# A planner that holds two engines for steps about to fall due, in a macaron encoder trunk on one core

## The chip, the cores and the metric

One core of one Trainium2 chip runs the whole program as one launch. The metric is the device time of an execution in microseconds (us), the median of several runs; the kernel before takes 918.53 us (three runs, 918.42 to 918.54). A core has five engines with an instruction queue each: TensorE (PE in the profile, its weight loads PEld), VectorE (DVE), ScalarE (ACT), GpSimd (POOL) and SyncE (SP, which here only issues DMAs). Each queue runs in its own order; semaphores hold an instruction until what it needs is there.

## The reference, cut to what matters

Two layers of a post-norm encoder on x of 1 x 256 x 1024 float32. Each layer is a SwiGLU, a mixer, a SwiGLU, each followed by a residual sum and a layer norm. The mixer of layer 0 is a bidirectional mLSTM with an output gate, that of layer 1 is windowed attention with 16 query heads on 4 key heads, a sink logit and a distance bias.

```python
def swiglu(x, w_in, w_out):                      # w_in 1024 x 5632, w_out 2816 x 1024
    gu = x @ w_in
    g, u = gu[..., :D_FF], gu[..., D_FF:]
    return (jax.nn.silu(g) * u) @ w_out
...
    p = x @ w_in                                 # mLSTM: q, k, v, o and the gates of both directions
...
    h = h_f + h_b                                # both directions, four heads of 256
    mu = jnp.mean(h, axis=-1, keepdims=True)
    var = jnp.mean(jnp.square(h - mu), axis=-1, keepdims=True)
    h = (h - mu) * lax.rsqrt(var + LN_EPS)
    h = h.transpose(0, 2, 1, 3).reshape(B, S, D_MODEL) * norm_g
    out = jax.nn.sigmoid(o.astype(jnp.float32)) * h
    return out.astype(x.dtype) @ w_out
...
for l in range(DEPTH):
    x = layer_norm(ALPHA * x + 0.5 * swiglu(x, ffn_w_in[l, 0], ffn_w_out[l, 0]), ...)
    x = layer_norm(ALPHA * x + mixer(x), ...)    # mLSTM for l = 0, attention for l = 1
    x = layer_norm(ALPHA * x + 0.5 * swiglu(x, ffn_w_in[l, 1], ffn_w_out[l, 1]), ...)
```

## The kernel before

**Arithmetic.** Every product of float32 matrices is made of three matmuls on a rounded part and its remainder: `mm3` (line 540) adds hi x hi, hi x lo and lo x hi. So each piece of a weight, a *word* of 128 partitions x 1024 numbers (512 KB), is loaded by `word` (493) on SP's queue and then split by `split` (502): ScalarE copies it to `w_hi`, VectorE subtracts to get `w_lo`. Activations are split in the same way when they leave PSUM (`split_evac`, 545). The 256 tokens are two tiles, t = 0 and 1.

**Stages.** `ffn`, `mlstm`, `ffn`, `ffn`, `attn`, `ffn`, each a function that writes down steps. An FFN does its first 768 hidden columns directly and the other 2048 in four *sevens* (`seven`, 844), each of which makes a 2 x 2 block product from seven products; some of their sums of words are made by DMAs that add (`bring`, issued by GpSimd), some by VectorE. All stages end in `tail` (650): the output projection, a residual sum, and the norm (`Norm`, 606), in which GpSimd takes a power for the column `rs`. The next stage is handed a `pending` that turns the normed x with the identity on TensorE (`to_xT`, 584) and splits it into `xT`.

**The head.** x is loaded in four quarters on ScalarE's queue (563), then ScalarE loads its table. TensorE turns the identity 14 times as a warm-up (`warm`, 592), turns the first quarter of x, warms up 8 times more and starts the first matmuls (`first_mm`, 725), between which the other quarters are turned. Steps for the sums of x that the sevens need (`x_sum`, named S) are made early, by VectorE and ScalarE. GpSimd works from the start on what it can: small loads of gates and sinks (`small_loads`, 572, issued by GpSimd), zeros, and the distance matrix of attention (`fwd`, `back`, `dist`), which takes four selects and an addition.

**The order of work.** Nothing of this is issued directly. `Book.note` writes each step down with what it depends on, `cost` gives it a duration, `latest` a due time (TensorE's own sequence laid end to end, and every other step as late as its users allow), and `sequence` (331) makes a list schedule: TensorE keeps the written order, the other four engines pick again and again. An engine's candidates are its 16 steps of earliest due time whose inputs are planned. Each has a time at which it could start (engine free, inputs there, a free slot), and the pick is:

```python
                soon = min(times)[0] + 1.0
                pick = min((x for x in times if x[0] <= soon), key=lambda x: x[1])
```

that is, of those that can start at once the one that is due first; an engine never idles while something can start. The planner's times decide only the order in each queue and which slot a tile takes. Slots are few: `HOMES` (line 29) has 10 for `w_hi`, 10 for `w_lo`, 16 for raw words and other big tiles, 8 PSUM banks.

**The mLSTM's end** (1124 to 1158). Four heads follow one another as `scores`, `mix`, `divide`, `settle`; `settle` normalizes a head's h, and its power is GpSimd's `hrs`. Between the heads stand the matmuls of the output gate, 32 units of three matmuls: 2 token tiles, 2 column halves m, 8 rows of blocks k. The eight gate words are indexed by (m, k // 2). The first four places, one a head, take token tile 0 with both halves, 4 units each; tile 1 follows in portions of 4, 4, 6 and 2. Then `gate_out` multiplies, `to_xT_banks` (a plain call of `to_xT`) turns h, and `tail` begins.

**Attention** (`attn`) interleaves, over 11 steps, `scores`, `scale`, `turn` and `values` of eight pairs of heads with pieces of projections. `values` sums into a bank that is emptied by the split into `q_hi` (ScalarE) and `q_lo` (VectorE).

Of the kernel before, what the change touches and what calls it, by code (L numbers as in the profile page):

```python
# [45 lines left out]
CT = [0, 1]  # L46

# [6 lines left out]
QUEUED = 6000.0  # L54

# [112 lines left out]
class Book:  # L168
# [162 lines left out]
    def sequence(self):  # L331
# [21 lines left out]
        dma = 0.0  # L353
# [20 lines left out]
        while len(given) < len(steps):  # L374
            best = None
            for e, list_ in todo.items():
# [7 lines left out]
                for n in cands:  # L384
                    s = steps[n]
                    t = max(free[e], ready[n])
                    if e == "SP":
                        t = max(t, dma - QUEUED)
                    t = homes(s, t)
                    if t is not None:  # L390
                        times.append((t, s.due, n))
                if not times:
                    continue
                soon = min(times)[0] + 1.0
                pick = min((x for x in times if x[0] <= soon), key=lambda x: x[1])
# [4 lines left out]
            s = steps[n]  # L400
# [10 lines left out]
            if e == "PE":  # L411
                at += 1
            else:
                todo[e].remove(n)
# [24 lines left out]
        self.given = given  # L439

# [13 lines left out]
def trunk_kernel(ctx: ExitStack, tc: tile.TileContext, x, ffn_w_in, ffn_w_out, ln_g, ln_b, ml_w_in, ml_gate_b,  # L454
# [24 lines left out]
    def bank(shape=(128, 512), name="pw"):  # L479
        return nc.tile(name, shape, "bank")  # L480
# [82 lines left out]
    for t, h in ((0, 0), (1, 0), (0, 1), (1, 1)):  # L563
        s_ = slice(h * 512, h * 512 + 512)
        nc.scalar.dma_start(xt[t][:, s_], x[0, t * 128:(t + 1) * 128, s_])
# [121 lines left out]
    def ffn(l, i, n, pending, last):  # L687
# [21 lines left out]
        if start:  # L709
            warm(14)  # L710
            to_xT(0, xt[0], (0,), nc.vector.tensor_copy)
# [4 lines left out]
        if start:  # L716
            gu(0)
            warm(8)
# [6 lines left out]
        def first_mm(ps, a):  # L725
# [5 lines left out]
            if a == 1:  # L731
                for t in range(2):
                    to_xT(t, xt[t], (1,))
# [211 lines left out]
    def mlstm(l, n, pending, last):  # L945
# [200 lines left out]
        to_xT_banks(0, flat[0])  # L1146
        wide_mm(po1[1], 1, wg, 1, range(6, 8))
        sigm(1, 1, po1[1])
        nc.scalar.preload_act_table(AF.Silu)
        for m in range(2):  # L1150
# [7 lines left out]
                    lambda: to_xT_banks(1, flat[1]))  # L1158

    def to_xT_banks(t, src):  # L1160
        to_xT(t, src)
# [219 lines left out]
```

## Time and profile before

| | |
|---|---|
| median of 3 runs | 918.53 us (918.42 to 918.54) |
| the profiled execution | 918.53 us, its span 916.8 us |
| granted TensorE clock | 0.997 |
| busy in the span | PE 904.0, DVE 810.7, ACT 584.5, POOL 144.3 us |
| DMA | 208.54 MB, mean 227 GB/s |

The profile is one execution. A timeline row gives start, duration, engine, line, operation, what is written and read (out<-in), shapes, how many such in a row, and in brackets how long the engine was idle before and what ended that. Since every step is issued from one line, all rows say L450, and the tiles' names tell them apart: `w_hi`, `w_lo` the parts of a word, `raw` and `b` words as loaded, `x` the tokens, `xT` the turned tokens, `S` the sums of x, `h` the mLSTM's output, `sc`, `pr` and `nse` scores, their turned form and their statistics in attention, `q` in attention also the result of a pair of heads. PE's durations overlap, as matmuls are pipelined, so starts are compared. A row of a stretch gives, after its length, busy time and count for PE, PEld, DVE, ACT and POOL, then the granted clock, the share of DMA time, and GB/s. A row of the list of waits gives who waited for whom: us in total, times, longest.

### The profile page before, as it was taken

How to read it: one execution, taken by the hardware profiler on the slowest of the kernel's cores; microseconds unless marked ns; L12 is line 12 of the kernel's file. 1: busy time of each engine (PE TensorE's matmuls, PEld its weight loads, DVE VectorE, ACT ScalarE, POOL GpSimd, SP SyncE). 2: the span in 40 equal slices, each digit the busy share in tenths (PEclk: the TensorE clock that was granted, in tenths of full speed). 3: DMA queues.
4: the chain of work that ended last, by engine and by line, in shares of the span. 5: the costliest groups of instructions: out<-in, count | busy, mean ns of one | idle time of the engine just before them, and what ended most of it. 6: DMA issues, size and time to landing. Idle time of an engine off the chain costs nothing.

```text
span 916.8 us, 12617 instructions
## 1 busy us (share of the span) xinstructions
PE 904.0 (99%) x4459; PEld 757.4 (83%) x4459; DVE 810.7 (88%) x985; ACT 584.5 (64%) x793; POOL 144.3 (16%) x177
## 2 busy tenths in 40 slices
PE   8999999999999999999999999999999999999996
PEld 7888888889988888888888888888898888888885
DVE  7989999887797989999889899997888698999985
ACT  6666777547564657776646667775488555677750
POOL 6112111005011021212011121210013202111100
PEclk9999999999999999999999999999999999999998
DMA  9998998944194688998965989989553367999831
GB/s 313 386 265 203 306 290 253 307 159 153 68 348 147 204 197 252 286 248 255 359 217 169 241 212 319 273 244 332 173 160 101 120 202 151 263 282 234 291 70 47
DMA packets 100704, 208.54 MB, mean 227 GB/s; under 512 B 6904, under 2 KB 21264, under 8 KB 100640
## 3 DMA queue, kind: packets, MB, share of 16 engines
q1 hardware_dynamic: 82368, 173.04, 53.7%
q0 software_dynamic: 17696, 33.65, 21.5%
q10 hardware_dynamic: 576, 1.05, 0.3%
q8 instruction: 35, 0.57, 0.2%
q14 instruction: 29, 0.24, 0.1%
HBM read 206.65 MB, written 1.05 MB: 227 GB/s over the span
## 4 chain that ended last, share of the span: by engine, by line
PE 94%; DVE 3%; ACT 1%; issue 1%; DMA 0%; DVEq 0%; ACTq 0%
PE pw L450 60%; PE py L450 34%; DVE w_lo L450 1%; DMA x<-in_x_dram 0%; ACT sc L450 0%; DVE x L450 0%; ACT w_hi L450 0%; DVE h L450 0%; ACT pr L450 0%; DVE pr L450 0%; DVE sc L450 0%; DVE few L450 0%; DVE xT_lo L450 0%; DVE hst L450 0%; DVE a_lo L450 0%
## 5 line engine op out<-in xcount | busy, mean ns | idle before, releaser
L450 ACT CAST w_hi<-b 128x1024 fp32r<-128x1024 f32 x224 | 234.2, 1056 | 88.1 <-PE py L450 44.5
L450 DVE TENSOR_TENSOR w_lo<-b,w_hi 128x1024 fp32r<-128x1024 f32 x224 | 267.1, 1218 | 17.6 <-ACT w_hi L450 17.1
L450 ACT CAST w_hi<-raw 128x1024 fp32r<-128x1024 f32 (+1 forms) x181 | 186.8, 1047 | 94.6 <-PE py L450 61.1
L450 DVE TENSOR_TENSOR w_lo<-raw,w_hi 128x1024 fp32r<-128x1024 f32 (+1 forms) x181 | 216.8, 1216 | 24.5 <-ACT w_hi L450 23.8
L450 PE MATMUL pw<-w_hi,xT_hi 128*128 128x512 f32 x480 | 189.5, 396 | 0.0
L450 PE MATMUL pw<-w_lo,xT_hi 128*128 128x512 f32 x480 | 186.5, 390 | 0.7 <-DVE w_lo L450 0.7
L450 PE MATMUL pw<-w_hi,xT_lo 128*128 128x512 f32 x480 | 187.0, 391 | 0.0
L450 PE MATMUL pw<-w_hi,S 128*128 128x512 f32 x512 | 162.9, 389 | 0.0
L450 POOL DMA_DIRECT2D b<-in_ffn_w_in_dram x64 | 77.3, 1210 | 457.7 <-DVE b L450 213.0
L450 PE MATMUL py<-w_hi,h_hi 128*128 128x512 f32 x317 | 125.2, 395 | 0.0
L450 PE MATMUL py<-w_hi,h_lo 128*128 128x512 f32 x317 | 123.8, 391 | 0.0
L450 PE MATMUL py<-w_lo,h_hi 128*128 128x512 f32 x317 | 123.5, 390 | 0.0
L450 PEld LDWEIGHTS pw<-w_hi,S 128*128 128x128 f32 x512 | 96.1, 188 | 20.0
L450 PEld LDWEIGHTS pw<-w_hi,xT_lo 128*128 128x128 f32 x480 | 90.0, 188 | 19.5 <-DVE xT_lo L450 0.3
L450 PEld LDWEIGHTS pw<-w_lo,xT_hi 128*128 128x128 f32 x480 | 90.3, 188 | 19.1 <-DVE w_lo L450 1.4
L450 PEld LDWEIGHTS pw<-w_hi,xT_hi 128*128 128x128 f32 x480 | 90.1, 188 | 17.3
L450 PE MATMUL pw<-w_lo,S 128*128 128x512 f32 x256 | 99.6, 389 | 0.0
L450 DVE TENSOR_TENSOR b<-b,b 128x1024 f32<-128x1024 f32 x64 | 78.1, 1221 | 2.0 <-DMA b<-in_ffn_w_in_dram 0.8
L450 PEld LDWEIGHTS py<-w_hi,h_lo 128*128 128x128 f32 x317 | 59.5, 188 | 13.2 <-DVE h_lo L450 0.7
L450 PEld LDWEIGHTS py<-w_lo,h_hi 128*128 128x128 f32 x317 | 59.6, 188 | 11.9
L450 PEld LDWEIGHTS py<-w_hi,h_hi 128*128 128x128 f32 x317 | 59.6, 188 | 11.6
L450 PEld LDWEIGHTS pw<-w_lo,S 128*128 128x128 f32 x256 | 48.1, 188 | 9.9
(198 smaller groups left out, 1076.2 us busy)
## 6 DMA issues: line engine op xcount, KB each, us to landing
b<-in_ffn_w_in_dram SPq DMA_DIRECT2D x128, 512.0 KB, 6.9
raw<-in_ffn_w_out_dram SPq DMA_DIRECT2D x88, 512.0 KB, 6.9
b<-in_ffn_w_in_dram POOLq DMA_DIRECT2D x64, 512.0 KB, 8.5
raw<-in_ffn_w_in_dram SPq DMA_DIRECT2D x32, 512.0 KB, 7.6
raw<-in_ml_w_in_dram SPq DMA_DIRECT2D x24, 512.0 KB, 8.6
raw<-in_ffn_w_in_dram SPq DMA_DIRECT2D x32, 256.0 KB, 6.1
raw<-in_at_w_in_dram SPq DMA_DIRECT2D x12, 512.0 KB, 8.4
raw<-in_ml_w_out_dram SPq DMA_DIRECT2D x8, 512.0 KB, 3.8
```

The source lines that it names most:

```text
L450: getattr(engines[s.engine], s.name)(*[real(x) for x in s.args], **{k: real(x) for k, x in s.kw.items()})
```

## The change

Five edits; the computation stays the same.

1. **Pressing steps.** For VectorE and ScalarE the pick goes through `wait_for`. If a step that is due earlier than the pick will be able to start before the pick would end (by more than 50 ns), and the pick would end later than that step's due time plus TensorE's present lateness less 500 ns, and the pick itself would not be made late by waiting, then the engine takes a step that ends by then (at most 60 ns over), or, if none does, stays idle for the pressing step.
2. **x on SP.** x's quarters are loaded on SP's queue, the same one as the words, written at the place where they are used: first quarter, first word, second quarter, then the second word and the last two. The warm-ups are 8 before the first turn of x and 14 after it.
3. **GpSimd late.** In the plan, a step of GpSimd other than an adding DMA does not start earlier than 25 us before it is due. This includes the small loads, the zeros and the distance matrix.
4. **The gate word by word.** The 32 units are listed anew: m = 0 for both tiles, word by word; then m = 1 for tile 0 and for tile 1. `GATE` says how many are taken at each place: 4 a head, 4 before the last `mix`, 10 after it, 2 after the turn of h's first tile.
5. `to_xT_banks` is replaced by the `to_xT` that it called.

```diff
+GATE = [4, 4, 4, 4, 4, 10, 2]
...
+PRESSING = 500.0
+EARLY = 25000.0
...
+                    if e == "POOL" and "accum_op" not in s.kw:
+                        t = max(t, s.due - EARLY)
...
-                soon = min(times)[0] + 1.0
-                pick = min((x for x in times if x[0] <= soon), key=lambda x: x[1])
+                now = min(times)[0]
+                open_ = [x for x in times if x[0] <= now + 1.0]
+                pick = min(open_, key=lambda x: x[1])
+                if e in ("DVE", "ACT"):
+                    pick = self.wait_for(times, open_, pick, now, late)
...
             if e == "PE":
                 at += 1
+                late = t - s.due
...
+    def wait_for(self, times, open_, pick, now, late):
+        steps = self.steps
+        takes = steps[pick[2]].takes
+        for u in sorted(times, key=lambda x: x[1]):
+            if u[1] >= pick[1]:
+                break
+            if now + 1.0 < u[0] < now + takes - 50.0 and now + takes > u[1] + late - PRESSING and (
+                    pick[1] + late > u[0] + steps[u[2]].takes + takes):
+                fits = [x for x in open_ if now + steps[x[2]].takes <= u[0] + 60.0]
+                return min(fits, key=lambda x: x[1]) if fits else u
+        return pick
...
-    for t, h in ((0, 0), (1, 0), (0, 1), (1, 1)):
+    def load_x(t, h):
         s_ = slice(h * 512, h * 512 + 512)
-        nc.scalar.dma_start(xt[t][:, s_], x[0, t * 128:(t + 1) * 128, s_])
+        nc.sync.dma_start(xt[t][:, s_], x[0, t * 128:(t + 1) * 128, s_])
+
+    load_x(0, 0)
...
         if start:
-            warm(14)
+            warm(8)
             to_xT(0, xt[0], (0,), nc.vector.tensor_copy)
...
             gu(0)
-            warm(8)
+            load_x(1, 0)
+            warm(14)
...
             if a == 1:
+                gu(1)
                 for t in range(2):
+                    load_x(t, 1)
                     to_xT(t, xt[t], (1,))
...
-        po = [bank(), bank()]
+        po = {}
+
+        def gate_units(n_):
+            for _ in range(n_):
+                t, m, k = units.pop(0)
+                if k == 0:
+                    po[t, m] = bank()
+                wide_mm(po[t, m], t, wg, m, (k,))
+                if k == 7:
+                    sigm(t, m, po[t, m])
+
+        units = [(t, 0, 2 * a + j) for a in range(4) for t in range(2) for j in range(2)]
+        units += [(t, 1, k) for t in range(2) for k in range(8)]
         nc.scalar.preload_act_table(AF.Sigmoid)
         for h in range(4):
-            wide_mm(po[h // 2], 0, wg, h // 2, range(4 * (h % 2), 4 * (h % 2) + 4))
+            gate_units(GATE[h])
             scores(h)
...
-        po1 = [bank(), bank()]
-        sigm(0, 0, po[0])
-        wide_mm(po1[0], 1, wg, 0, range(4))
+        gate_units(GATE[4])
         mix(3)
-        sigm(0, 1, po[1])
-        wide_mm(po1[0], 1, wg, 0, range(4, 8))
         divide(3)
         settle(3)
+        gate_units(GATE[5])
         for m in range(2):
             gate_out(0, m)
-        sigm(1, 0, po1[0])
-        wide_mm(po1[1], 1, wg, 1, range(6))
-        to_xT_banks(0, flat[0])
-        wide_mm(po1[1], 1, wg, 1, range(6, 8))
-        sigm(1, 1, po1[1])
+        to_xT(0, flat[0])
+        gate_units(GATE[6])
```

More of the change, by code (lines that the diff above doesn't have):

```diff
@@ L352, in sequence @@
         free = {e: 0.0 for e in todo}
-        dma = 0.0
+        dma = late = 0.0
         given = []
@@ L1157, in mlstm @@
         return tail(y, lambda c, t: pair(xT, A, c, tok(t)), (todo, todo), True, norm, last, 4,
-                    lambda: to_xT_banks(1, flat[1]))
-    def to_xT_banks(t, src):
-        to_xT(t, src)
+                    lambda: to_xT(1, flat[1]))
     def attn(l, n, pending, last):
```

## The prediction

> **What bounds the kernel.** I read the page first, then the list of who waited for whom on TensorE, then stretches of the span, and last the timelines around each wait that the list names.
>
> ```profile
> span 916.8 us, 12617 instructions
> PE 904.0 (99%) x4459; PEld 757.4 (83%) x4459; DVE 810.7 (88%) x985; ACT 584.5 (64%) x793; POOL 144.3 (16%) x177
> ```
>
> The profiled execution took 918.53 us, the same as the median of the three runs, so 1.7 us lie outside its span and the sum below can be made on the span and carried over unchanged. TensorE is idle for 916.8 - 904.0 = 12.8 us. A change that leaves the matmuls alone, as this one does, can only win from those.
>
> ```profile
> 57.73 5.44 PE pw L450 x24
> PE py L450 <- DVE ident L450: 1.7, 1, 1.7
> PE pw L450 <- DVE q_lo L450: 1.2, 2, 0.8
> PE pw L450 <- ACT pr L450: 0.7, 1, 0.7
> PE pw L450 <- DVE w_lo L450: 0.7, 1, 0.7
> PE py L450 <- DVE h L450: 0.5, 1, 0.5
> PE py L450 <- DVE xT_lo L450: 0.4, 1, 0.4
> PE py L450 <- DMA x<-in_x_dram: 0.3, 1, 0.3
> ```
>
> The first line is a piece of the chain that ended last, inside an FFN: 24 matmuls in 5.44 us, 0.227 us from start to start. That is the pace everything else is held against. The other seven are all of TensorE's waits. Two belong to the first 6 us. The other five are short, and they lie in three places: the head, the end of the mLSTM, the attention. The long FFN stretches have none. What the change can be worth is the sum of these five, with what each costs around its idle time.
>
> **The head.** Here four edits meet: x on SP's queue, warm-up split 8 and 14 for 14 and 8, GpSimd's work put off, the pressing rule.
>
> ```profile
> 1.72 3.25 PE L450 MATMUL py<-ident 128*128 128x128 f32 x14 [1.72 <-DVE ident L450]
> 5.23 1.12 PE L450 MATMUL py<-ident,x 128*128 128x128 f32 x4 [0.27 <-DMA x<-in_x_dram]
> 6.14 1.42 PE L450 MATMUL py<-ident 128*128 128x128 f32 x8
> 7.31 0.71 PE L450 MATMUL pw<-w_hi,xT_hi 128*128 128x512 f32 x2
> 7.86 0.64 PE L450 MATMUL py<-ident,x 128*128 128x128 f32 x4
> 8.26 0.70 PE L450 MATMUL pw<-w_hi,xT_lo 128*128 128x512 f32 x2
> 14.40 0.39 PE L450 MATMUL pw<-w_hi,xT_hi 128*128 128x512 f32 x1
> 15.44 0.50 PE L450 MATMUL pw<-w_lo,xT_hi 128*128 128x512 f32 x1 [0.65 <-DVE w_lo L450]
> 5.63 1.14 ACT L450 CAST w_hi<-raw 128x512 fp32r<-128x512 f32 x2 [0.99 <-DMA raw<-in_ffn_w_in_dram]
> 4.00:5.00 1.00, 0.96 (x5) 0.56 (x3) 0.00 (x0) 0.64 (x1) 0.69 (x3) 1.00 1.05 395
> ```
>
> Of x and the first word, x's quarter is now sent alone and the word behind it. Both together are 0.262 + 0.524 MB, and both orders have moved them by the time ScalarE now starts on the word, 5.63. So the word gains nothing, and freeing ScalarE of four issues gains nothing either, since it already sat 0.99 us waiting for that word. The quarter gains the time of the word: 0.524 MB at 395 GB/s (the stretch's last column) are 1.33 us, so it is there near 4.3 instead of 5.2.
>
> The other three quarters of x and the later words now stand in one order on SP; the engines move 395 GB/s whoever issues, so I take 0 for the words behind them.
>
> TensorE cannot use the earlier quarter. Four early transposes took 6.14 - 5.23 = 0.91 us, 0.228 each; four later ones 8.26 - 7.86 = 0.40, 0.10 each. The eight warm-ups took 7.31 - 6.14 = 1.17, which is three slow and five fast, so the rate changed near 6.8. After the change: transposes from 4.3 to 5.2, then 14 warm-ups that stand ahead of the first matmul in order: seven slow ones to 6.8, seven fast ones to 7.5. The first matmul starts 0.2 later than at 7.31. From both sides: 0.1 earlier if x lands as the eight warm-ups end (3.6, below), 1.1 later if all 14 stay slow (5.2 + 3.2 = 8.4).
>
> The stall further on is what can go. From 14.40 to 15.44 is 1.04 us for a step of 0.227, so 0.81 are lost.
>
> ```profile
> 10.11 1.64 DVE L450 TENSOR_TENSOR w_lo<-raw,w_hi 128x1024 fp32r<-128x1024 f32 x1 [0.26 <-ACT w_hi L450]
> 13.46 0.67 DVE L450 TENSOR_TENSOR S<-x,py 128x512 f32<-128x512 f32 x1
> 14.05 2.46 DVE L450 TENSOR_TENSOR w_lo<-raw,w_hi 128x1024 fp32r<-128x1024 f32 x2
> 9.35 1.32 POOL L450 TENSOR_SCALAR_AFFINE_SELECT fwd<-fwd 128x512 f32<-128x512 f32 x2
> L450 DVE TENSOR_TENSOR w_lo<-raw,w_hi x181: 681/1218/1635, 7.7 to 888.0; 128x1024 fp32r<-128x1024 f32 x179, 128x512 fp32r<-128x512 f32 x2
> 178.03 1.48 POOL L450 TENSOR_TENSOR rs<-rs,few 128x1 f32<-128x1 f32 x1 [29.80 <-DVE rs L450]
> ```
>
> VectorE took a sum S of no hurry (0.67) just ahead of the w_lo that TensorE stood waiting for, and an earlier w_lo took 1.64 instead of the median 1.218 beside GpSimd's select. Either repair, 0.42 or 0.67, covers most of 0.81, and the two together all of it. Head: -0.8 + 0.2 = **-0.6**.
>
> GpSimd's work is not saved, only put off to 25 us before it is due: the memsets and small loads for the mLSTM come shortly before 178.03, the selects and the addition for attention's distances some 25 us ahead of that stage. GpSimd's queue is in order, its loads included: behind the moved work stand the norms' rs, for which the next stage's x waits. The last row shows 29.80 us without work before such an rs, so I take nothing; without that cover an rs comes late by the pieces in front of it, 1.32 us for a pair of selects.
>
> At their new place the reading operations can hit VectorE as the select did: 0.42 each, five such (four selects, one addition), 0 to 2.1 us, hidden as long as VectorE runs ahead there. I take 0, since TensorE has no wait in the list before attention's own. [...]
>
> **The mLSTM's end.** The word-by-word order uses each of the first four gate words for both token tiles at once.
>
> ```profile
> 266.22 0.60 PE L450 MATMUL py<-ident,h 128*128 128x128 f32 x4
> 267.32 0.63 PE L450 MATMUL py<-ident,h 128*128 128x128 f32 x4 [0.50 <-DVE h L450]
> 269.41 0.39 PE L450 MATMUL py<-w_lo,xT_hi 128*128 128x512 f32 x1
> 270.22 0.50 PE L450 MATMUL py<-w_hi,xT_lo 128*128 128x512 f32 x1 [0.42 <-DVE xT_lo L450]
> 263.64 2.48 DVE L450 SCALAR_TENSOR_TENSOR w_lo<-raw,few,w_hi 128x1024 fp32r<-128x1024 f32 x2
> 267.09 2.48 DVE L450 SCALAR_TENSOR_TENSOR w_lo<-raw,few,w_hi 128x1024 fp32r<-128x1024 f32 x2
> 240.00:256.00 16.00, 16.00 (x106) 14.64 (x105) 12.24 (x34) 6.89 (x21) 1.44 (x2) 1.00 0.38 131
> 256.00:270.00 14.00, 13.30 (x71) 10.94 (x69) 13.84 (x28) 11.10 (x18) 3.33 (x2) 1.00 1.00 353
> ```
>
> Lost: 267.32 - 266.22 - 0.40 = 0.70, and 270.22 - 269.41 - 0.227 = 0.58, together 1.28. Both times VectorE was on a pair of w_lo of the output projection (2.48 us, to 266.1 and 269.6) when h or xT_lo came up. Why so late: all eight gate words are split early and stay live until token tile 1 has used them, which is 8 of 10 slots for hi and for lo. So VectorE idles 16.00 - 12.24 = 3.76 us in the first stretch and is full (13.84 of 14.00) in the second. In the new order one word is done with after each head, four slots come free by the end of the heads, and up to three splits (3.76 / 1.24) move into the idle time. Matmuls between the last mix and the transposes stay 10 units of three, 10 x 3 x 0.227 = 6.8 us of cover; the last four gate words, which were split before, must now be ready within them, and they take the slots freed. That is 3.7 us of relief for 1.28 us of stall: I take **-1.2**, between -1.3 and +0.7 (the first stall doubled, if those four words come late).
>
> **Attention.**
>
> ```profile
> 696.19 1.03 ACT L450 CAST w_hi<-raw 128x1024 fp32r<-128x1024 f32 x1
> 697.25 1.23 DVE L450 TENSOR_TENSOR w_lo<-raw,w_hi 128x1024 fp32r<-128x1024 f32 x1 [0.97 <-ACT w_hi L450]
> 698.40 0.42 DVE L450 TENSOR_TENSOR q_lo<-pw,q_hi 128x256 fp32r<-128x256 f32 x1
> 698.87 0.66 PE L450 MATMUL pw<-ident,sc 128*128 128x128 f32 x4 [0.80 <-DVE q_lo L450]
> 711.50 0.51 ACT L450 ACTIVATE sc<-sc,nse 128x256 f32<-128x256 f32 x1 [1.28 <-DVE nse L450]
> ```
>
> ScalarE begins a w_hi at 696.19 and VectorE its w_lo at 697.25, so q_lo, which frees the bank that TensorE wants, starts at 698.40. This is the case the new rule is written for: leave the long split, take the short step that is about to be ready, and even idle for it. Without the w_lo in front, q_lo starts up to 698.40 - 697.25 = 1.15 us earlier, more than the 0.80. What is queued behind the rule's waiting is that same w_lo, and TensorE's products with its word. Both q_lo waits, 1.2 in the list: **-1.2** (0 to -1.2). I leave the 0.7 on pr: there ScalarE itself idled 1.28 us for VectorE and the pr stood behind, an order made from planned durations that the chip did not keep. The last 0.7 can go too, or double.
>
> **Elsewhere** the FFNs have nothing to win; I charge +0.2 for the rule's idling.
>
> Sum: -0.6 - 1.2 - 1.2 + 0.2 = **-2.8**, span 914.0, time 918.53 - 2.8 = **915.7 us**.
>
> **Rivals.** *The plan's relief stays in the plan.* The rule acts on planned times; the row at 711.50 shows plan and chip apart by 1.28 us, more than most of these stalls. Then only what follows from the data flow comes, the gate words: -1.2, 917.3 us. Against it: the two q_lo stalls and the S ahead of w_lo are the plan's own choices, seen as such in the trace.
>
> *The clock comes later.* TensorE now idles from 1.72 + 8 x 3.25 / 14 = 3.6 to 4.3, against 0.27 before. The fast rate came 6.8 - 1.72 = 5.1 us after the first warm-up. If that count starts anew at 4.3, fast is 9.4: first matmul at 8.4, then 1.0 us at half rate, 0.5 lost; 8.4 - 7.31 + 0.5 = 1.6 instead of 0.2, so 915.7 + 1.4 = 917.1 us. For: the longer idle; against: x00 may be earlier, and 0.7 is short beside 5.1. [...]
>
> *VectorE idles itself into the bound: slower.* In the FFN's sevens there is little to idle with:
>
> ```profile
> 85.89:116.78 30.89, 30.89 (x142) 25.57 (x141) 29.62 (x30) 22.20 (x25) 4.82 (x5) 1.00 0.94 272
> ```
>
> One seven leaves VectorE 30.89 - 29.62 = 1.27 us, and the planner books a split at (1024 + 71) / 0.96 = 1.14 us where the trace has 1.218, so it believes in more. Waiting beyond 1.27 us in a seven falls on TensorE. Two waits of 0.9 (the rule allows up to a split less 0.05) are 1.8, 0.53 too many, in 16 sevens 8.5 us: 924.2 us. Against: the rule first looks for a step that fits, and does not wait if the split itself would be late.
>
> **Chances.** Forecast 0.49; relief in the plan only 0.27; clock 0.12; VectorE idling 0.12. A measurement of this kernel can tell about 0.2%, 1.84 us. The forecast is faster than that, the next two lie within it unless other gains come on top (0.06 of their 0.39), the last is slower: 0.55, 0.33, 0.12. Lower end 914.2: all five waits gone at no charge are 0.81 + 1.28 + 1.2 + 0.7 = 4.0, and 0.3 more if attention's cost more than their idle time, as the head's did (0.81 for 0.65). Upper end 918.6: the 917.3 of the first rival with one rs late by 1.3. Left out are the slower case and a tail.
>
> **What would show it.** Right: q_lo gone from TensorE's waits, the w_lo of the output projection spread over the heads, VectorE below 13.84 of 14 before the mLSTM's transposes, no 1.64 in the head, first matmul near 7.5. Wrong: slow transposes past 8 us; a new TensorE wait for w_lo inside an FFN; rs late with POOL busy ahead of it; the same waits at the same places.

## The result, and the profile after

The changed kernel takes 914.09 us (median of 5 runs, 913.66 to 914.60) against 918.53 (5 runs, 918.38 to 918.54): a ratio of 0.9952, 95% interval 0.9938 to 0.9967, so 4.44 us less, beyond the 0.2% that a measurement of this kernel can tell. The forecast was 915.7 with 914.2 to 918.6: the direction holds, the gain is 1.6 us larger than forecast, and the median lies 0.1 us below the lower end. The profiled execution of the changed kernel took 913.72 us.

The page's first lines and the whole list of TensorE's waits:

```profile
span 911.8 us, 12602 instructions
PE 902.6 (99%) x4459; PEld 757.3 (83%) x4459; DVE 811.4 (89%) x985; ACT 584.2 (64%) x793; POOL 145.4 (16%) x177
```

```profile
engine line waited for: us in total, times, longest us
PE py L472 <- DVE ident L472: 1.7, 1, 1.7
```

All engines do the work they did before. TensorE's idle time fell from 12.8 to 911.8 - 902.6 = 9.2 us, and of the list of seven only the wait for the identity at the very start is left. Idle time is 3.6 of the span's 5.0 us. The other 1.4 are busy time (904.0 to 902.6), which the prediction had put out of reach: the first matmul after a wait is longer than its neighbours (0.50 against 0.39 us in the rows of before), and the early transposes run at two rates, below.

**The head.** TensorE's timeline of the changed kernel (start, duration, operation, and the idle time ahead of it in brackets):

```profile
1.71 1.97 PE L472 MATMUL py<-ident 128*128 128x128 f32 x8 [1.71 <-DVE ident L472]
3.77 1.11 PE L472 MATMUL py<-ident,x 128*128 128x128 f32 x4
4.67 2.31 PE L472 MATMUL py<-ident 128*128 128x128 f32 x14
6.74 0.71 PE L472 MATMUL pw<-w_hi,xT_hi 128*128 128x512 f32 x2
...
13.66 0.39 PE L472 MATMUL pw<-w_hi,xT_hi 128*128 128x512 f32 x1
13.89 0.39 PE L472 MATMUL pw<-w_lo,xT_hi 128*128 128x512 f32 x1
```

x's first quarter is there at 3.77, not near 4.3, and TensorE hardly waits for it. The first matmul starts at 6.74 (7.31 before, 7.5 forecast). The product that came at 15.44 behind the stall comes at 13.89, 0.23 behind its neighbour: the stall is gone, and the head is 1.55 us shorter, not 0.6.

**The mLSTM's end.** The two stretches that the prediction quoted, and the transposes of h in TensorE's timeline, which now run in one piece:

```profile
240.00:256.00 16.00, 16.00 (x103) 14.48 (x102) 15.30 (x36) 9.44 (x27) 1.82 (x2) 1.00 0.75 239
256.00:270.00 14.00, 14.00 (x74) 11.87 (x73) 13.66 (x33) 9.21 (x15) 1.70 (x2) 1.00 0.94 320
```

```profile
264.37 1.04 PE L472 MATMUL py<-ident,h 128*128 128x128 f32 x8
266.86 0.39 PE L472 MATMUL py<-w_lo,xT_hi 128*128 128x512 f32 x1
267.09 0.40 PE L472 MATMUL py<-w_hi,xT_lo 128*128 128x512 f32 x1
```

VectorE (the third busy number) went from 12.24 to 15.30 of 16.00 in the first stretch: the splits moved forward as forecast. The second transpose group and the product behind xT_lo lost 0.72 and 0.61 us against their neighbours of before; both are given back, 1.33 together against 1.2 forecast.

**Attention.** TensorE where it waited for q_lo, then ScalarE and VectorE at the same place:

```profile
694.67 0.28 PE L472 MATMUL pw<-kT_hi,q_lo 64*128 64x256 f32 x2
694.88 0.66 PE L472 MATMUL pw<-ident,sc 128*128 128x128 f32 x4
```

```profile
693.07 1.03 ACT L472 CAST w_hi<-raw 128x1024 fp32r<-128x1024 f32 x1
694.39 0.42 DVE L472 TENSOR_TENSOR q_lo<-pw,q_hi 128x256 fp32r<-128x256 f32 x1 [1.23 <-ACT q_hi L472]
694.74 1.22 DVE L472 TENSOR_TENSOR w_lo<-raw,w_hi 128x1024 fp32r<-128x1024 f32 x1
```

This is the rule at work: VectorE idles 1.23 us, the last 0.3 of them with a split at hand (its `w_hi` was ready at 693.07 + 1.03 = 694.10), does q_lo, then the split; before, VectorE idled 0.97 us for `w_hi` and the split stood first. Both q_lo waits went (1.26 us), and the wait for pr as well (0.99 with what followed it), which the forecast had kept. ScalarE's rows for pr, before and in the changed kernel, show why:

```profile
713.00 0.56 ACT L450 CAST pr<-pw 128x512 fp32r<-128x512 f32 x1
706.27 1.20 ACT L472 CAST pr<-pw 128x512 fp32r<-128x512 f32 x2
```

Before, the second pr stood behind three steps on `sc` that had waited 1.28 us for VectorE (the row at 711.50 in the prediction). Now both stand ahead of such steps, the next of which starts at 708.07.

Two places got worse. The last pair's scores now wait for GpSimd's scaling. TensorE's and GpSimd's rows:

```profile
713.84 1.92 PE L472 MATMUL pw<-ident,sc 128*128 128x128 f32 x8
715.52 0.47 PE L472 MATMUL py<-w_hi,q_hi 128*128 128x512 f32 x1
```

```profile
713.11 1.84 POOL L472 TENSOR_SCALAR sc<-sc,nse 128x256 f32<-128x256 f32 x4 [4.02 <-DVE nse L472]
```

Eight transposes take 715.52 - 713.84 = 1.68 us here, where the eight of h above take 265.16 - 264.37 = 0.79 (the next product stands at 265.16): 0.89 us given back, in gaps of 0.12 us, too short for the list of waits. And at attention's entry GpSimd's postponed selects and the addition run beside VectorE. First VectorE in the kernel before, with GpSimd's addition where it stood before, then VectorE and GpSimd in the changed kernel:

```profile
12.99 1.31 POOL L450 TENSOR_TENSOR dist<-fwd,back 128x512 f32<-128x512 f32 x1
650.16 1.28 DVE L450 SCALAR_TENSOR_TENSOR x<-x,rs,ln_b 128x1024 f32<-128x1024 f32 x1
651.36 2.36 DVE L450 TENSOR_TENSOR w_lo<-raw,w_hi 128x1024 fp32r<-128x1024 f32 x2
653.97 1.22 DVE L450 TENSOR_TENSOR w_lo<-raw,w_hi 128x1024 fp32r<-128x1024 f32 x1
```

```profile
646.91 1.64 DVE L472 SCALAR_TENSOR_TENSOR x<-x,rs,ln_b 128x1024 f32<-128x1024 f32 x1
648.48 3.19 DVE L472 TENSOR_TENSOR w_lo<-raw,w_hi 128x1024 fp32r<-128x1024 f32 x2
651.92 1.97 DVE L472 TENSOR_TENSOR w_lo<-raw,w_hi 128x1024 fp32r<-128x1024 f32 x1
```

```profile
647.43 1.60 POOL L472 TENSOR_SCALAR_AFFINE_SELECT fwd<-fwd 128x512 f32<-128x512 f32 x1
648.99 1.60 POOL L472 TENSOR_SCALAR_AFFINE_SELECT back<-back 128x512 f32<-128x512 f32 x1
650.67 2.13 POOL L472 TENSOR_TENSOR dist<-fwd,back 128x512 f32<-128x512 f32 x1
```

VectorE loses 0.36 + 0.83 + 0.75 = 1.94 us, close to the 2.1 that the prediction gave as the upper bound. TensorE loses 0.6 us there against before: 0.2 at its first products near 642.6, and 0.4 near 654.5, where it stands for xT_lo (0.27) and then for the next product. Both are gone in f2_nopool and f2_again below, which differ from the changed kernel by GpSimd's lateness alone.

The operations of GpSimd are longer there as well: each of the two selects shown takes 1.60 us against 0.63 in the head of before (the pair at 9.35 us), the addition 2.13 against 1.31 (the first row above). Both engines are slower there; what makes them so was not shown.

### The profile page after: what moved, and what is told of

Read it like the earlier page. It is cut to its first block, busy times and chain, and to the rows that moved or that the text cites. A ratio compares the mean times of both kernels' runs of the same rounds, so it can differ in the third digit from the quotient of the medians.

```text
span 911.8 us, 12602 instructions
## 1 busy us (share of the span) xinstructions
PE 902.6 (99%) x4459; PEld 757.3 (83%) x4459; DVE 811.4 (89%) x985; ACT 584.2 (64%) x793; POOL 145.4 (16%) x177
## 4 chain that ended last, share of the span: by engine, by line
PE 93%; DVE 3%; ACT 1%; issue 1%; POOL 0%; DMA 0%; DVEq 0%; POOLq 0%
PE pw L472 60%; PE py L472 33%; DVE w_lo L472 1%; DVE x L472 1%; ACT sc L472 1%; DVE pr L472 0%; DMA x<-in_x_dram 0%; DVE stats L472 0%; ACT pr L472 0%; ACT w_hi L472 0%; POOL sc L472 0%; DVE xT_lo L472 0%; DVE sc L472 0%; DVE few L472 0%; POOL rs L472 0%
```

## The experiments

My theory after this comparison: each edit works in its own stage, the word-by-word gates in the mLSTM, x's landing at the start, the pressing rule in head and attention, GpSimd's lateness for the head and against attention's entry. The rival: the edits overlap, one of them does most of it. The table has all runs. "Head" is the start of the product that stood behind the stall (15.44 us in before), "rest" the time from there to the start of the last matmul, both in the profiled execution; "turn" is the start of the first transpose after the last slow one (0.21 us apart before it, 0.11 after). The ratio is to runs of the kernel before that were made along with each kernel (their medians are 918.44 to 918.53).

| kernel | us, median (range, runs) | ratio, 95% interval | turn | head | rest |
|---|---|---|---|---|---|
| before | 918.53 (918.38 to 918.54, 5) | | 6.78 | 15.44 | 893.64 |
| the whole change | 914.09 (913.66 to 914.60, 5) | 0.9938 to 0.9967 | 5.95 | 13.89 | 890.60 |
| e1_gate | 917.41 (917.33 to 917.61, 11) | 0.9980 to 0.9998 | 6.86 | 15.50 | 893.11 |
| e2_head | 918.45 (917.62 to 918.71, 11) | 0.9988 to 1.0006 | 6.68 | 15.46 | 893.75 |
| e3_press | 914.52 (914.43 to 914.68, 5) | 0.9944 to 0.9971 | 6.68 | 14.54 | 891.00 |
| e4_pool | 919.32 (918.67 to 920.95, 11) | 1.0006 to 1.0023 | 4.54 | 14.99 | 894.82 |
| f1_nopress | 917.05 (916.63 to 917.46, 11) | 0.9976 to 0.9994 | 7.55 | 15.60 | 892.73 |
| f2_nopool | 913.16 (912.85 to 915.28, 5) | 0.9936 to 0.9961 | 7.27 | 16.12 | 890.15 |
| f2_again | 913.74 (912.94 to 913.89, 5) | 0.9934 to 0.9959 | 6.44 | 14.76 | 889.97 |
| f3_warm | 913.80 (913.56 to 914.03, 5) | 0.9937 to 0.9962 | 4.54 | 13.74 | 890.62 |
| a_again | 914.12 (913.65 to 914.67, 5) | 0.9940 to 0.9965 | 7.52 | 14.88 | 890.58 |
| g1_scale | 913.38 (913.07 to 913.72, 5) | 0.9933 to 0.9958 | 5.24 | 14.56 | 890.07 |
| g3_scale_warm_pool | 913.14 (912.32 to 913.89, 5) | 0.9925 to 0.9952 | 6.03 | 15.35 | 889.54 |
| g4_scale_warm | 913.31 (913.06 to 913.46, 5) | 0.9931 to 0.9956 | 7.10 | 14.36 | 889.85 |
| f5_nohead | 913.90 (913.66 to 914.11, 5) | 0.9937 to 0.9964 | 4.75 | 13.72 | 890.68 |
| f6_nogate | 914.18 (913.84 to 915.32, 5) | 0.9943 to 0.9968 | 7.81 | 15.26 | 890.88 |

Two things bear on every row. In e4_pool, f1_nopress and f6_nogate no further transpose follows at once, so the turn is later than the number: 4.92, 8.28 and 8.32 by the record of the granted clock in the traces. And from the start of the last matmul to the end the span takes 7.7 us in before and e2_head, 7.3 in the other fourteen profiles: the other kernels have 0.43 us from there, whatever their edit.

### Each edit alone, on the kernel before

**e1_gate**: only the gates' order.

```diff
-            wide_mm(po[h // 2], 0, wg, h // 2, range(4 * (h % 2), 4 * (h % 2) + 4))
+            gate_units(GATE[h])
```

> The kernel before with the output gates of the mLSTM cut into word-by-word units, and nothing else. Theory (each edit acts in its own stage): the two TensorE waits in the mLSTM, which took 0.72 and 0.61 us more in before than in the changed kernel, go with the gates' order, since units of the gates fill the places where TensorE waited for the heads' powers; the time falls by 1.3 us, to 917.2, and head and attention stay as in before. Rival (the pressing rule did it: ScalarE's powers fell from 1.67 to 0.78 us of delay because engines kept time for them): the waits stay, the time stays within 0.3 us of 918.5.

Measured: 1.0 us gained, 1.3 expected, and 0.43 of it at the very end; in the mLSTM TensorE gained 0.6. The wait for h went, that for xT_lo stayed. Its TensorE rows of the head and of the mLSTM:

```profile
15.50 0.50 PE L451 MATMUL pw<-w_lo,xT_hi 128*128 128x512 f32 x1 [1.01 <-DVE w_lo L451]
...
266.26 1.04 PE L451 MATMUL py<-ident,h 128*128 128x128 f32 x8
...
269.68 0.50 PE L451 MATMUL py<-w_hi,xT_lo 128*128 128x512 f32 x1 [0.54 <-DVE xT_lo L451]
```

The first row tells something more. In this execution x landed 0.35 us earlier than in before's profile and the first matmul started at 7.16 instead of 7.31, with the head's code unchanged, and still the product came at 15.50: what is won ahead of the stall is lost in the stall (1.01 us of idle time instead of 0.65). In these executions VectorE sets the end of the head.

**e2_head**: only x on SP's queue, and 8 and 14 warm-ups.

```diff
-        nc.scalar.dma_start(xt[t][:, s_], x[0, t * 128:(t + 1) * 128, s_])
+        nc.sync.dma_start(xt[t][:, s_], x[0, t * 128:(t + 1) * 128, s_])
-            warm(14)
+            warm(8)
```

> The kernel before with the head's edit alone: x on SyncE's queue in order of use, and 8 and 14 warming matmuls in place of 14 and 8. The changed kernel ran the head 1.55 us earlier. Theory (x's landing, at 3.72 instead of 5.18, is worth only the start; the rest of the head is set by VectorE's and ScalarE's order, which the pressing rule and GpSimd's lateness change): the first matmul of the first layer comes 0.5 us earlier, but the wait of 0.8 us at 14.4 us stays, so that 0.3 to 0.6 us are gained: 918.0. Rival (the landing sets the whole head): 1.5 us are gained, 917.0, and the wait at 14.4 us is gone too.

Measured: no difference by the medians (918.45 and 918.45), but the eleven times fall into two groups, 917.62 to 917.78 (five) and 918.45 to 918.71 (six), where those of before lie at 918.40 to 918.73. The profile is one of the second group. Its TensorE rows:

```profile
4.07 1.12 PE L450 MATMUL py<-ident,x 128*128 128x128 f32 x4 [0.38 <-DMA x<-in_x_dram]
4.97 2.60 PE L450 MATMUL py<-ident 128*128 128x128 f32 x14
7.33 0.70 PE L450 MATMUL pw<-w_hi,xT_hi 128*128 128x512 f32 x2
...
15.46 0.50 PE L450 MATMUL pw<-w_lo,xT_hi 128*128 128x512 f32 x1 [0.83 <-DVE w_lo L450]
```

In this execution x is there 1.2 us earlier and nothing follows: the 14 warm-ups fill the time, as the prediction said, and the stall takes the rest. The rival's 917.0 was not reached. What made five executions 0.8 us shorter is not known, since none of them was profiled, so the edit's worth on the kernel before stays open between 0 and 0.8.

**e3_press**: only the planner's rule (the function that the change adds and its call).

```diff
+                if e in ("DVE", "ACT"):
+                    pick = self.wait_for(times, open_, pick, now, late)
```

> The kernel before with the planner's new rule for VectorE and ScalarE alone. Theory: it removes the waits for q_lo in the attention (0.88 and 0.38 us in before), most of those for pr (0.74 and 0.25) and the 0.8 us at 14.4 us, and does nothing to the first matmul; some 0.9 us come back as waits for GpSimd's scaled scores near 715 us: 2 us are gained, 916.5. Rival (the planner's own prices are off by more than the rule's 0.5 us, so that the relief stays on paper): within 0.4 us of 918.5, and the q_lo waits are still in the list.

Measured: 3.9 us gained, twice the theory's 2, nearly all that the whole change gains; without the 0.43 at the very end it is 3.5. All of TensorE's waits:

```profile
PE py L468 <- DVE ident L468: 1.7, 1, 1.7
PE py L468 <- DVE xT_lo L468: 0.4, 1, 0.4
PE pw L468 <- DVE w_lo L468: 0.2, 1, 0.2
```

Beyond the waits named in the theory, the one for h in the mLSTM is gone (0.5 us gained there), which I had put down to the gates. TensorE also gained 0.13 to 0.18 us at the end of each of the first three FFNs and at the start of the last one, 0.6 together; f1_nopress, without the rule, has none of it to speak of. The 0.9 us back at GpSimd's scaling near 715 are there as expected: the rule brings out that wait, not the lateness.

**e4_pool**: only GpSimd's lateness.

```diff
+                    if e == "POOL" and "accum_op" not in s.kw:
+                        t = max(t, s.due - EARLY)
```

> The kernel before with GpSimd's early work held until 25 us ahead of its due time, and nothing else. Theory: GpSimd's index and mask work leaves the first 15 us, in which one w_lo of VectorE took 1.64 us beside it and takes 1.23 without, so the wait at 14.4 us shrinks by 0.4; and it comes up at 646 to 653 us beside VectorE's x and w_lo steps, which costs 0.3 us there: within 0.3 us of 918.5. Rival (GpSimd's work never touched the path): the wait at 14.4 us stays 0.8 us and the attention's entry stays too. Rival (the late work hits harder): over 1 us lost at 640 to 660 us.

Measured: 0.9 us lost by the medians, more than the theory's bound of 0.3, less than the second rival's, and elsewhere. Here too the times fall into two groups, 918.67 to 919.32 (six) and 920.33 to 920.95 (five); the profile is of the first, at 918.98. The product behind the head's stall came 0.45 us earlier, the size expected, though the wait itself was no shorter (0.79 us), as TensorE's turn was early. The loss in the profile is in the mLSTM, where the plan, made anew, put one more scaled split ahead of the last head. TensorE's and VectorE's rows there:

```profile
268.43 0.63 PE L453 MATMUL py<-ident,h 128*128 128x128 f32 x4 [2.12 <-DVE h L453]
```

```profile
261.70 1.28 DVE L453 SCALAR_TENSOR_TENSOR w_lo<-raw,few,w_hi 128x1024 fp32r<-128x1024 f32 x1
262.89 0.87 DVE L453 SCALAR_TENSOR_TENSOR h<-py,den,h 128x256 f32<-128x256 f32 x2
```

In before the h step started at 261.78 with that split behind it; here it starts 1.1 us later, and the wait for h is 2.12 us in place of 0.50. A change of times anywhere in the plan can reorder a stage that was not touched.

### The whole change with one edit left out

**f1_nopress**: without the call of the rule.

```diff
-                if e in ("DVE", "ACT"):
-                    pick = self.wait_for(times, open_, pick, now, late)
```

> The changed kernel without the planner's new rule for VectorE and ScalarE; x, warming, GpSimd and gates as changed. Theory (the rule alone took 3.9 us, the rest together 0.5): the q_lo waits are back near 695 and 702 us, the wait for w_lo near 14 us too, while the mLSTM stays without waits for h and xT_lo: 917.6 to 918.3. Rival (the edits overlap, so that what the rule removes the others remove too): under 916.5.

Measured: 917.05, so that the rule is worth 914.1 to 917.05 = 2.9 us within the whole, below the theory's range by 0.5 us, far from the rival. Those of attention are the waits of before, the one for w_lo is half as long:

```profile
PE pw L470 <- DVE q_lo L470: 1.2, 2, 0.8
PE pw L470 <- ACT pr L470: 0.7, 1, 0.7
PE pw L470 <- DVE w_lo L470: 0.3, 1, 0.3
```

The mLSTM's waits do not come back: without the rule the other three edits clear them, while the rule alone (e3_press) cleared one.

**f2_nopool** and, for a second profile, **f2_again**: without GpSimd's lateness.

```diff
-                    if e == "POOL" and "accum_op" not in s.kw:
-                        t = max(t, s.due - EARLY)
```

> The changed kernel with GpSimd's work as early as before, all else as changed. Theory (GpSimd beside VectorE costs in both places): one w_lo of the head takes 1.64 us again and a wait of 0.3 to 0.6 us for w_lo is back near 14 us; the wait for xT_lo near 654 us, 0.27 us, is gone: 914.1 to 914.5. Rival (lateness is a plain loss, as the 0.9 us by which the kernel before grew with it alone would have it): 913.3. Rival (the head needs it wholly): 915.0.

> The changed kernel with GpSimd's work as early as before, once more, since its five times lay at 912.85 to 914.06 and at 915.28, and its profile, at 915.28, had the turn of TensorE's rate at 7.27 us and a wait of 1.05 us for w_lo at 14.85. Theory (early GpSimd work delays VectorE in the head, which matters when TensorE's turn is late, and saves some 0.4 us at 654 us): 912.8 where the turn comes by 6 us, 915 where it comes after 7, median near 913.5. Rival (lateness of GpSimd is a plain loss of 0.9 us): median 913.2 and no stall in the head at any turn.

Measured: nine of ten times from 912.85 to 914.06, one at 915.28, medians 913.16 and 913.74, against 914.09 and 914.12 with the lateness. In both profiles the rest is shorter by 0.4 to 0.6 us, because the 0.6 us at attention's entry are gone; the head is longer, 14.76 at a turn of 6.44 and 16.12 at 7.27, against 14.88 at 7.52 with the lateness. So both sides of the trade are real, as the theory had it, and the lateness looks like a loss of some 0.4 us (the medians of ten times are 913.7 and 914.1), which is less than the intervals can tell. The theory's 912.8 for an early turn was not seen in a profile. The head of f2_nopool is so long because a split on VectorE stood 1.03 us for ScalarE's `w_hi` (at 14.39), and that cast had stood 0.84 us for its word to land (at 13.30). In f2_again ScalarE made the same cast at 12.23 without such a wait. Why the word landed late was not found.

**f5_nohead**: with x on ScalarE's queue and 14 and 8 warm-ups again.

```diff
-        nc.sync.dma_start(xt[t][:, s_], x[0, t * 128:(t + 1) * 128, s_])
+        nc.scalar.dma_start(xt[t][:, s_], x[0, t * 128:(t + 1) * 128, s_])
```

> The changed kernel with x on ScalarE's queue and 14 and 8 warming matmuls, as in before; rule, GpSimd and gates as changed. Theory (the head is a race of two chains, x to TensorE's turn and VectorE's splits; with the splits relieved, x's landing near 5 us instead of 3.8 is what is late): the second word's first product with w_lo comes at 14.3 to 14.6 us in place of 13.9 to 14.9, with no wait for w_lo, the time is 0.3 to 0.6 us longer, 914.5. Rival (x's landing never mattered, only VectorE's stall): 914.1, as the whole change.

Measured: 913.90, the head at 13.72. The rival holds: the head edit is worth nothing here, within what the intervals can tell. So the head's gain came from the rule and the late GpSimd work, which together take VectorE off the path there; with one of them alone a wait for w_lo is left in e3_press (0.2 us), f1_nopress (0.3) and one of the two profiles without the lateness (0.9).

**f6_nogate**: with the gates in their old order.

```diff
-            gate_units(GATE[h])
+            wide_mm(po[h // 2], 0, wg, h // 2, range(4 * (h % 2), 4 * (h % 2) + 4))
```

> The changed kernel with the output gates in their old order, all else as changed. Theory (late GpSimd work let one more scaled split slip ahead of the last head's steps in the kernel before, and the gates' order keeps it away): the waits for h or xT_lo are back near 264 to 268 us, 0.6 to 1.3 us, 915.1. Rival (the rule alone removes them): within 0.3 us of 914.1.

Measured: 914.18; the rest is 0.3 us longer than in the whole change, and of the waits only 0.15 us for h is back. The rival holds: with the rule and the late GpSimd work there, the gates' order adds at most 0.3.

### Where the spread of 1 us comes from

**a_again**: the changed kernel unaltered, for a second profile.

> The changed kernel once more, unaltered, for a second profile beside its times. TensorE's transposes of 213 ns turned into ones of 105 ns at anything from 4.7 to 8.5 us in the profiles so far, and the changed kernel's runs spread over 0.9 us where those of before spread over 0.3. Theory (in the changed kernel the head is bound by TensorE, so that the moment of that turn passes into the time, half of each us by which it comes later): the times lie again between 913.4 and 915.0, and this profile's time differs from the other's 913.72 by half the difference of its turn to 5.95 us. Rival (the spread has its source elsewhere): profiles with unlike turns have like times, or the difference arises behind 20 us.

Its TensorE rows:

```profile
4.05 1.12 PE L472 MATMUL py<-ident,x 128*128 128x128 f32 x4 [0.37 <-DMA x<-in_x_dram]
4.96 3.00 PE L472 MATMUL py<-ident 128*128 128x128 f32 x14
7.72 0.71 PE L472 MATMUL pw<-w_hi,xT_hi 128*128 128x512 f32 x2
...
14.88 0.39 PE L472 MATMUL pw<-w_lo,xT_hi 128*128 128x512 f32 x1
```

The same 14 warm-ups last 7.72 - 4.96 = 2.76 us here and 6.74 - 4.67 = 2.07 in the other profile: at 0.213 us for a slow one and 0.107 for a fast one, twelve slow ones against six. The turn came at 7.52 instead of 5.95, the first matmul at 7.72 instead of 6.74, the head ends 0.99 us later, the rest is the same to 0.02 us, and the time is 914.67 against 913.72. So the difference of 0.95 us between two executions of one kernel is all in the head, and with TensorE now the head's bound, the moment of the turn and x's landing (0.28 us later here) pass into the time. Six more slow transposes at 0.106 us extra are 0.64, and the one during which the rate turned took 0.06 more (0.17 us); with the landing's 0.28 that makes 0.98, as measured at the first matmul. The turn's part, 0.70, is a little under half of 1.57, as the theory had it.

An early turn does not always pass on. In g1_scale it came at 5.24, but ScalarE began on the first word only at 6.42 (5.58 and 5.50 in the two profiles here), TensorE stood 0.58 us for its `w_hi`, and the head ended at 14.56. The first word is the next bound.

**f3_warm**: 14 and 8 warm-ups in place of 8 and 14.

```diff
-            warm(8)
+            warm(14)
...
-            warm(14)
+            warm(8)
```

> The changed kernel with 14 warming matmuls ahead of x's first transposes and 8 behind, as before had them. x lands at 3.72 us in the changed kernel and TensorE waits 0.4 us for it behind the eighth warming matmul; fourteen of them end at 4.8. Theory (the first matmul comes when all 26 transposes have run, whatever their order): that wait goes, the first matmul comes at 6.4 instead of 6.74, 0.3 us gained: 913.8. Rival (the order was changed for its own sake): x's transposes end 1 us later, their copies to xT_hi and xT_lo follow, and the first matmul comes at 7.2: 914.6. Rival (neither decides): within 0.15 us of 914.1.

Measured: 913.80, as the theory said, with the first matmul at 6.24. But the turn of this profile was an early one, and f5_nohead shows the same head; the difference of 0.3 us to the changed kernel's medians of 914.1 lies inside the spread of its ten times (913.65 to 914.67) and does not settle the edit's worth.

### A version faster than both

**g1_scale**: two of the last pair's four scaling steps go to VectorE. **g4_scale_warm** adds f3_warm's order, **g3_scale_warm_pool** also GpSimd's early work.

```diff
+                    e = nc.vector if j == 7 and a == 1 else nc.gpsimd
-                    nc.gpsimd.tensor_scalar(sc[j, t][:, a], sc[j, t][:, a], sm[:, t, a:a + 1], 1.0,
+                    e.tensor_scalar(sc[j, t][:, a], sc[j, t][:, a], sm[:, t, a:a + 1], 1.0,
```

> The changed kernel with two of the four steps that scale the last pair's scores moved from GpSimd to VectorE. In the changed kernel GpSimd's four steps take 1.84 us in a row and TensorE stands 0.14, 0.34 and 0.34 us behind them near 714 us. Theory: those waits go, 0.8 us gained, 913.3. Rival (VectorE's own work for the same pair, q_lo and pr, comes later by the two steps, and the waits move there): within 0.3 us of 914.1, with a wait for q_lo or pr in the list.

> Two of these edits, GpSimd late as in the changed kernel: two of the last pair's scaling steps on VectorE, and 14 and 8 warming matmuls. Theory: the times add to 913.1, with TensorE's wait for xT_lo at 654 us left, and a spread of less than 1 us. Rival (warming matters only by the moment at which TensorE's rate turns in a given run): 913.4 as with the scaling steps alone.

> Three edits to the changed kernel together: GpSimd's work as early as before, two of the last pair's four scaling steps on VectorE, and 14 and 8 warming matmuls. By the times of each alone (913.16, 913.38 and 913.80 against 914.09) the theory that they add gives 912.2. Rival (the head stall of early GpSimd work returns): 913 to 914.

Measured: 913.38, 913.31 and 913.14. In g1_scale the eight transposes take 715.63 - 714.55 = 1.08 us instead of 1.68, by its TensorE rows:

```profile
714.55 1.33 PE L472 MATMUL pw<-ident,sc 128*128 128x128 f32 x8
715.63 0.47 PE L472 MATMUL py<-w_hi,q_hi 128*128 128x512 f32 x1
```

The waits did not move to q_lo or pr; the gain is 0.5 us by the rest and 0.7 by the medians, a little under the theory's 0.8, and the rival is out. The five times of g4_scale_warm lie below all ten of the changed kernel, and the warm-ups add nothing that can be told over g1_scale. The 0.8 us are under 0.1%, less than the intervals can tell. g3_scale_warm_pool has the shortest rest (889.54) and a long head (15.35), its times from 912.32 to 913.89: the theory that all three add (912.2) fails by 0.9, the rival's 913 to 914 holds.

## Why the prediction was right and where it was wrong

The main mechanism was right: five short waits of TensorE for VectorE and ScalarE, which the change removes. Two terms of the sum were badly mis-sized, and one was not there. Held against the two profiles of the changed kernel (the first at 913.72, a_again at 914.67):

| term | forecast, us | measured, us |
|---|---|---|
| head | -0.6 | -1.55 and -0.56 |
| mLSTM | -1.2 | -1.33, and 0.1 in the product behind: -1.4 |
| attention | -1.2 | entry +0.6, then -0.1; q_lo -1.2, pr -1.0, scaling +0.9: -0.85 |
| elsewhere | +0.2 | -0.75 and -0.9 |
| behind the last matmul | not there | -0.43 |
| outside the span | 0 | +0.2 |
| sum | -2.8 | -4.8 and -3.9; the median -4.4 |

- **The step that failed first is "Elsewhere".** "the FFNs have nothing to win; I charge +0.2 for the rule's idling": measured -0.75 and -0.9, an error of about 1 us in both profiles, with the wrong sign. It was read off the list of waits, which shows no idle time as short as 0.12 us. At 166.6 us, for instance, the step from the last product to the transposes of `e` took 0.32 us before and 0.23 in the changed kernel, and the list of before has nothing there. These gains of 0.1 to 0.2 at a time lie at the ends of the first three FFNs, at the start of the last, and in the product behind the head's stall; the first four come with the rule (e3_press against f1_nopress). No idling of VectorE fell on TensorE in an FFN.
- **The second is the head's first matmul.** "The rate changed near 6.8" was read off one execution and taken as a fixed moment, so the first matmul was put at 7.5 and 0.2 us were charged. The turn is not fixed: it came between 4.67 and 8.32 us in the sixteen profiles. The first matmul came at 6.74 in one execution of the changed kernel and at 7.72 in the other; the stall's 0.8 was right in both. That a_again's head comes out at the forecast's number is luck: its first matmul is 0.2 us later than forecast, and the products up to the stall went 0.15 faster. The arithmetic had a slip as well: x's quarter, 1.33 us earlier than 5.2, is there at 3.9 and not at 4.3 (measured 3.77 and 4.05); by the prediction's own steps that puts the first matmul near 7.3, with no charge.
- **The end** was no term of the sum. The 0.43 us lie behind the landing of the results, in the program's closing: GpSimd's last drain starts 0.36 us after its last signal and lasts 0.24 in before, 0.07 and 0.09 in the changed kernel. The cause was not tried.
- **The lower end** of the range, 914.2, was built from the five waits alone, so it left out all three. The 0.43 at the end alone are more than the 0.1 by which the median lies below it.
- **mLSTM**: the size is right, the credit is not. The word order does move the splits forward, as forecast (VectorE is busy 14.52 of the 16 us from 240 in e1_gate, 12.44 in e3_press, 12.24 in before), but it is not needed for the gain. The rule alone and the word order alone each remove the wait for h, and each leaves the one for xT_lo; the late GpSimd work alone removes that one and lengthens the one for h. Any two of the three clear both, but for 0.15 us in f6_nogate.
- **Attention**: q_lo as worked out. That pr would stay was wrong, by 1.0; it went with the same rule (e3_press), by the new order on ScalarE shown above. GpSimd's scaling took nearly all of that back, a wait that the forecast did not name; it comes with the rule too.
- **GpSimd late** was taken at 0 for attention's entry, with 0 to 2.1 as bounds for VectorE: 1.94 of VectorE, 0.6 of TensorE. That it can cost more by reordering a stage it does not touch (e4_pool, 0.9 us) was not seen.
- **x and the first word**: that the word gains nothing held (ScalarE starts on it at 5.58, against 5.63 before). The words behind lost nothing either: 2.33 MB were moved by 9 us in the changed kernel, 2.25 in before. Against the 395 GB/s that the forecast took whoever issues, SP's queue alone moved 389 from 13 to 16 us in before, and in the changed kernel 333 from 4 to 7 us and 395 from 8 to 16. That TensorE can't use the earlier quarter held in e2_head's profile and, within the whole change, in f5_nohead.
- **The rivals.** Relief that stays in the plan: no, the rule's plan held on the chip (e3_press). The clock that comes later: it can't be dismissed. Seven profiles have a gap of 0.2 to 0.4 us ahead of x's first transposes, and the full rate comes at 6.50 to 8.32 in them; in the nine without it comes at 4.67 to 7.20. With such a gap the turn came 1.5 us later on average, though no count of 5.1 us started anew behind it: in before the turn comes 1.7 us behind the gap. No run tested the gap alone. VectorE idling into the bound: no TensorE wait in any FFN.

## What to carry to other kernels

Where TensorE is 99% busy, look at what stands directly ahead of each short wait on the slower engine: here letting a short step that is about to be ready go before a long one took 2.9 (left out of the whole change) to 3.5 us (alone) of 4.4, and edits aimed at the same waits hardly added to it. A list of waits has a smallest entry, and many slips below it can add up to as much as the entries. Before you price an earlier start, find out which engine sets the end of that stage; while VectorE held the head, 1.2 us of earlier input were worth nothing in the execution that was profiled. A moment that the program does not fix, such as TensorE's turn to its fast rate, needs more than one profile, and goes into the range.

## What the runs showed of the hardware

- TensorE's transposes turned from 0.213 to 0.107 us apart, and the traces' record of the granted clock puts the change to the full rate at 4.67 (f3_warm) to 8.32 us (f6_nogate) in the sixteen profiles, 3.0 to 6.6 us after the first transpose at 1.7. Two executions of one kernel have it at 5.93 and 7.64, of another at 7.27 and 6.50. In all sixteen the stretch at full rate lasts 901.12 (the changed kernel, first profile), 904.53 (before) or 907.95 us. The first two differ by 3.413 us, and the three are 264, 265 and 266 times that: in these profiles the clock changed on a grid of 3.41 us, and where on the grid an execution began differed from one to the next. The column of the granted clock in the rows of a stretch does not show the slow start: it reads 1.00 from 4 us on in before and in the changed kernel.
- At attention's entry a VectorE step beside GpSimd's selects or addition took 1.64 us in the changed kernel instead of the 1.28 of before, a pair 3.19 instead of 2.36, one 1.97 instead of 1.22. GpSimd's select took 1.60 us there and 0.63 at 9.35 us in before, its addition 2.13 and 1.31.
- The times of two kernels fall into two groups, 0.8 us apart in e2_head and 1.5 in e4_pool. Each has a profile of one group only; what sets the other was not found.
